# Rotary halves swapped by transfers, and norm factors spread through DRAM, in a fused attention, state-space and expert layer

## The chip, the cores and the metric

The kernel runs on one NeuronCore of a Trainium2 chip. Time is device microseconds (us) of one execution; less is better. The engines named below are TensorE (PE, with its weight loads as PEld), VectorE (DVE), ScalarE (ACT), GpSimd (POOL) and SyncE (SP), which here only issues transfers.

## The reference, cut to what matters

One decoder layer over 512 tokens of width 1024. The part that the change touches is the latent attention: two RMS norms of narrow latents, and a rotary embedding of queries and keys.

```python
def rms_norm(x, g):
    xf = x.astype(jnp.float32)
    return (xf * lax.rsqrt(jnp.mean(xf * xf, -1, keepdims=True) + NORM_EPS) * g).astype(x.dtype)

def apply_rope(x, cos, sin):
    x1, x2 = jnp.split(x.astype(jnp.float32), 2, axis=-1)
    return jnp.concatenate([x1 * cos - x2 * sin, x2 * cos + x1 * sin], axis=-1).astype(x.dtype)

def mla_heads(q_lat, kv_lat, k_pe, cos, sin, q_norm_g, w_q_b, kv_norm_g, w_kv_b):
    q = (rms_norm(q_lat, q_norm_g) @ w_q_b).reshape(B, S, MLA_HEADS, MLA_NOPE_DIM + MLA_ROPE_DIM)
    q_nope = q[..., :MLA_NOPE_DIM]
    q_pe = apply_rope(q[..., MLA_NOPE_DIM:], cos[:, None], sin[:, None])
    kv = (rms_norm(kv_lat, kv_norm_g) @ w_kv_b).reshape(B, S, MLA_HEADS, MLA_NOPE_DIM + MLA_V_DIM)
    k_nope, v = kv[..., :MLA_NOPE_DIM], kv[..., MLA_NOPE_DIM:]
    k_pe = apply_rope(k_pe, cos, sin)
    ...   # scores = q_nope k_nope + q_pe k_pe, causal softmax, times v
```

The rest of the layer: a LayerNorm, one input projection, a causal convolution, a chunked state-space product (SSD, 16 heads), an output projection, a second LayerNorm, and an expert mixer (PEER) over 16,384 experts. There are 8 attention heads, each with 128 plain and 64 rotary features.

## The kernel before, in words

Everything is written as an instruction order by hand: each engine runs its own queue in the order of the code, and waits on semaphores only. Activations lie with features on the 128 partitions and the 512 tokens along a row. Weights stream in by SP as raw tiles `wir`; ACT rounds each to a high part `wih` (L122), DVE or POOL subtracts for the low part `wil` (L132), and each product is three matmuls (L85, L86, L87: high by high, low by high, high by low).

The stages that matter here, with their places in the profiled execution:

- **Input projection (to 137 us).** The loop over `i` makes 18 blocks of 128 features in PSUM tiles `pa`. Block 0 holds the rotary key (rows 0 to 63 of `kd`) and the time steps; blocks 1 to 12 go through the convolution on DVE (L388, L390); blocks 13 to 15 are the query latent, 16 and 17 the key/value latent. At `i == 3`, `k_rope` makes the rotary key: two matmuls with 0/1 matrices (L600, L601) put the key twice over the partitions, plain and with its halves swapped, and `rope` (L593 to L595 on DVE) multiplies by cosine and sine and adds.
- **Latent norms.** `lat_a(15)` and `lat_a(17)` sum squares over the partitions with a matmul that leaves one factor for each token, token on partition, and take the inverse root on DVE (a chain of twelve small operations). Four DVE operations (L659) spread the factors on a diagonal, and in `lat_b` a matmul with ones (L664) copies them to every partition. `lat_b` then scales each latent block on DVE (L667), rounds on ACT (L669) and subtracts on DVE (L670).
- **Gate projection (the loop over `n`, 137 to 195 us).** Eight weight tiles make `zt`. Between them stands work of the state-space part (`do`): `ssd_s` makes states (L544, read by DVE at L546), `ssd_off` their outputs (L518, read by DVE at L521), `ssd_y` the products inside a chunk (L530, read at L534). All of their PSUM results are four rotating tiles `pb`.
- **Attention (from 198 us).** A pair of heads `p` takes its rotary queries from `q_pe(p)`, a generator with two halves. The first makes a product in a PSUM tile and scales it into `qx` (L752 on ACT for pair 0, L750 on DVE for the others). The second, in `before`, multiplies `qx` by a permutation matrix (L756), runs `rope` (L593 to L595), rounds on ACT into `qph` (L760) and subtracts into `qpl` on DVE (L761); POOL then copies both into the operands `q` by four transfers (L764). `scores` reads them at L814, for pair `p` first at head `2p`. Thirty-nine steps `st` run the heads one after the other, four query blocks each: `scores`, DVE's row maximum (L818), ACT's exponential (L826), scaling, transposes (L845), an evacuation by ACT and DVE (L736 `thh`, L737 `thl`) and the product with `v` (`po`). Each step also advances the generator of the next heads' operands once.

The names `pt`, `pu`, `po` are PSUM tiles of the attention.

Of the kernel before, what the change touches and what calls it, by code (L numbers as in the profile page):

```python
# [11 lines left out]
F32 = mybir.dt.float32  # L12
# [6 lines left out]
OP = mybir.AluOpType  # L19
# [4 lines left out]
S = 512  # L24
D = 1024
NB = 4
# [30 lines left out]
BIG = 1.5 * 2.0 ** 26  # L57
GG = 48 - UG // 8

C_COS, C_SIN, C_PQ, C_END = 0, 512, 1024, 1152  # L60
T_TRI, T_DK, T_RK, T_END = 0, 128, 256, 384

P_CW, P_CB, P_LG, P_LB, P_QG, P_KG, P_SG, P_END = 0, 48, 60, 68, 76, 79, 81, 89

# [2 lines left out]
def tile_block(ctx: ExitStack, tc: tile.TileContext, I, out):  # L67
    nc = tc.nc
    ctx.enter_context(tc.manual_schedule())
    V, A, T, G = nc.vector, nc.scalar, nc.tensor, nc.gpsimd  # L70
# [141 lines left out]
    C = cs2.tile([128, C_END], F32, name="C")  # L212
    PAR = cs2.tile([128, P_END], F32, name="PAR")
    HR = cs2.tile([128, 48], F32, name="HR")
    ident = cs2.tile([128, 128], F32, name="ident")
# [12 lines left out]
    dram = pool("dram", space=DRAM)  # L228
    xsp = dram.tile([NB, 128, D], F32, name="xsp")
    gsp = dram.tile([NT // 32, 128, 128, 32], F32, name="gsp")  # L230
    acd = dram.tile([64, 128], F32, name="acd")
    asp = dram.tile([PRE - KEEP, 128, NU], F32, name="asp")

    wst = pool("wst")
# [6 lines left out]
    wk = pool("wk")  # L241
    CT = wk.tile([128, T_END], F32, name="CT")
    tri = CT[:, T_TRI:T_TRI + 128]
    ntm = wk.tile([128, 128], BF16, name="ntm")
    ones = wk.tile([128, 128], F32, name="ones")
# [7 lines left out]
    pb = lambda: psB.tile([128, 512], F32, name="pb")  # L253
# [48 lines left out]
    for p in range(2):  # L302
# [7 lines left out]
        rs = sqrt_rs(lnp, mv4[:, bs, 1], [128, 2], f"l{p}", eps)  # L310
# [57 lines left out]
    kd = wk.tile([128, S], F32, name="kd")  # L368
# [10 lines left out]
    cu, co = {}, {}  # L379
# [211 lines left out]
    def rope(pool_, px, prot, tag, bufs):  # L591
        a = pool_.tile([128, S], F32, name=tag, bufs=bufs)
        V.tensor_tensor(a, px, cosT, op=OP.mult)  # L593
        V.tensor_tensor(prot, prot, sinT, op=OP.mult)
        V.tensor_tensor(a, a, prot, op=OP.add)  # L595
        return a

    def k_rope():
        p1, p2 = pb(), pb()
        T.matmul(p1, CT[0:64, T_DK:T_DK + 128], kd[0:64], start=True, stop=True)  # L600
        T.matmul(p2, CT[0:64, T_RK:T_RK + 128], kd[0:64], start=True, stop=True)  # L601
        kr = rope(wk, p1, p2, "co", 2)
        A.activation(kpe[0], kr, AF.Copy)
        V.tensor_tensor(kpe[1], kr, kpe[0], op=OP.subtract)

    dp = dt_prep()
    for i in range(13):
        ps = proj(i)
        if i == 0:
            A.activation(kd[0:80], ps[0:80], AF.Copy)  # L610
        else:
            conv_a(i, ps)
        if i >= 2:
            conv_b(i - 1)
        if i >= 5:
            conv_c(i - 2)
        if i in (4, 5):
            conv_c(i - 3)
        if i in (2, 4, 6, 7, 9):
            next(dp)  # L620
        if i == 3:
            k_rope()
        if i == 11:
            ssd_m(0, 0)
        if i == 12:
            ssd_cb(0)
            ssd_m(0, 1)
# [19 lines left out]
    sqs, lrs = {}, {}  # L647

    def lat_a(i):
        m = 3 if i == 15 else 2  # L650
        ps = pb()
        for b in range(NB):
            T.matmul(ps[:, b:b + 1], sqs[i][:, b * 128:(b + 1) * 128], ones[:, 0:1], start=True, stop=True)
        v = lat.tile([128, NB], F32, name="lv", bufs=2)
        V.tensor_scalar(v, ps[:, 0:NB], 1.0 / (128 * m), EPS, op0=OP.mult, op1=OP.add)
        rs = rsqrt(lat, v, [128, NB], "ls")
        dg = wk.tile([128, S], F32, name="co", bufs=2)
        for b in range(NB):
            V.tensor_scalar(dg[:, b * 128:(b + 1) * 128], ident, rs[:, b:b + 1], None, op0=OP.mult)  # L659
        lrs[i] = dg  # L660

    def lat_b(i):
        ps = pb()
        T.matmul(ps, ones, lrs[i], start=True, stop=True)  # L664
        lo, hi, g0, oh, ol = (0, 3, P_QG, qlh, qll) if i == 15 else (3, 5, P_KG, kvh, kvl)
        for m in range(lo, hi):
            V.scalar_tensor_tensor(qraw[m], qraw[m], PAR[:, g0 + m - lo:g0 + m - lo + 1], ps,  # L667
                                   op0=OP.mult, op1=OP.mult)
            A.activation(oh[:, m - lo], qraw[m], AF.Copy)  # L669
            V.tensor_tensor(ol[:, m - lo], qraw[m], oh[:, m - lo], op=OP.subtract)  # L670

    for i in range(13, 18):
        ps = proj(i)
        if i == 16:
            lat_a(15)
        q = qraw[i - 13] = wk.tile([128, S], F32, name="qr", bufs=5)
        A.activation(q, ps, AF.Copy)
        sqs[i] = wk.tile([128, S], F32, name="ca", bufs=3)
        A.activation(sqs[i], ps, AF.Square)
        if i not in (13, 16):  # L680
            V.tensor_tensor(sqs[i], sqs[i], sqs[i - 1], op=OP.add)
        do(i - 13)
        if i == 17:
            lat_b(15)


    for n in range(8):
        hf, kp = divmod(n, 4)
        if kp == 0:
            acc = [pa() for _ in range(4)]  # L690
        h, l = item()
        for kk in range(2):
            k = kp * 2 + kk
            wh, wl = h[:, kk * 512:(kk + 1) * 512], l[:, kk * 512:(kk + 1) * 512]
            for b in range(NB):
                bs = slice(b * 128, (b + 1) * 128)
                mm3(acc[b], HH[:, k, bs], HL[:, k, bs], wh, wl, k == 0, k == 7)
        if kp == 3:
            for b in range(NB):
                A.activation(zt[:, b, hf * 512:(hf + 1) * 512], acc[b], AF.Silu)  # L700
        if n == 1:
            lat_a(17)
        if n == 4:
            lat_b(17)
        do(n + 5)
# [23 lines left out]
    pp = pu  # L729
# [12 lines left out]
    def q_pe(p):  # L742
        wh, wl = item()
        ps = pp()
        for k in range(3):
            ks = slice(k * 128, k * 128 + 128)
            mm3(ps, wh[:, ks], wl[:, ks], qlh[:, k], qll[:, k], k == 0, k == 2)
        qx = ml.tile([128, S], F32, name="qx")
        if p:
            V.tensor_scalar(qx, ps, SCALE, None, op0=OP.mult)  # L750
        else:
            A.activation(qx, ps, AF.Copy, scale=SCALE)  # L752
        win.splits(cnt[0] + 1)
        yield
        pr = pp()
        T.matmul(pr, C[:, C_PQ:C_PQ + 128], qx, start=True, stop=True)  # L756
        a = rope(ml, qx, pr, "rp", 1)
        q2 = [ml.tile([128, S], F32R, name=f"q2{e}", bufs=2) for e in range(2)]
        qp = [ml.tile([128, S], F32R, name="qp" + n) for n in "hl"]
        A.activation(qp[0], a, AF.Copy)  # L760
        V.tensor_tensor(qp[1], a, qp[0], op=OP.subtract)  # L761
        for e in range(2):
            for x in (e, 1 - e):
                G.dma_start(q2[e][x * 64:x * 64 + 64], qp[e ^ x][e * 64:e * 64 + 64])  # L764
            QP[2 * p + e] = q2[e]
# [107 lines left out]
            w_out_mm(acc, b, k, hl)  # L873

    gq, gk = q_pe(0), qk_nope(0, pk=pt)
    for g in (gq, gk, gq, gk, gk):
        next(g, None)
    g = chain(qk_nope(1, pq=pt), v_proj(0))
    for _ in range(2):
# [919 lines left out]
def _host(inp):  # L1799
# [31 lines left out]
    ch[:, 0:256] = np.repeat(r, 2)  # L1831
    ch[:, 256:512] = np.repeat(np.arange(16), 16)
    o["ch"] = ch
    rot = (r // 64) * 64 + (r % 64 + 32) % 64
    c[rot, C_PQ + r] = 1
    c1[r % 64, T_DK + r] = 1
    c1[rot % 64, T_RK + r] = 1
    o["cst1"] = c1
    inv = (10000.0 ** (-np.arange(32) / 32.0)).astype(f)
    ang = (np.arange(S, dtype=f)[:, None] * inv).astype(np.float64)  # L1840
# [37 lines left out]
```

## Time and profile before

| what | value |
|---|---|
| median of 3 runs | 1547.5 us (1543.41 to 1547.81) |
| the profiled execution | 1544.92 us, of which the span is 1543.0 us |
| granted TensorE clock, mean | 0.998 |
| busy share of the span | PE 99%, PEld 87%, DVE 88%, ACT 49%, POOL 41% |
| chain that ended last | PE 83%, DVE 7%, DMA 4%, ACT 3% |

The busy share says how much of the span an engine had an instruction in flight; matmuls overlap, so 99% is not a statement that nothing waited. The chain that ended last is followed back from the last instruction, at each step to what released it.

### The profile page before, as it was taken

The page shows a single profiled execution, that of the slowest core. Times are in us where ns is not written, and L with a number is a line of the kernel's source. Part 1 is how long each engine was busy: PE and PEld are TensorE (multiplying, and loading weights), DVE is VectorE, ACT ScalarE, POOL GpSimd, SP SyncE. Part 2 cuts the span into 40 slices and gives each one's busy share as a digit, 9 for nine tenths or more (in the row PEclk, how much of TensorE's full clock was granted, in tenths as well). Part 3 has the DMA queues.
Part 4 walks back from the last instruction along what each step waited for, and adds up shares of the span by engine and source line. Part 5 has one row for each costly group of instructions (what it writes and reads, how often), then busy time and mean ns, then how long its engine had stood idle before and what let it go on. Part 6 is the DMA issues. An engine that isn't in the chain of part 4 may idle for free.

```text
span 1543.0 us, 24619 instructions
## 1 busy us (share of the span) xinstructions
PE 1522.6 (99%) x8696; PEld 1338.1 (87%) x8696; DVE 1354.0 (88%) x2611; ACT 761.2 (49%) x1415; POOL 634.6 (41%) x466
## 2 busy tenths in 40 slices
PE   9999999999999999999999999999999999999997
PEld 7787888888888999999999889999999888888885
DVE  8979768655799999999998599988999999999997
ACT  5574476742333444667667544444443344444442
POOL 0000032420044522435430476656666766776610
PEclk9999999999999999999999999999999999999999
DMA  6242122375322566999998999999999999999983
GB/s 258 96 149 99 57 71 59 104 252 164 127 76 90 150 209 215 346 343 348 383 329 288 366 402 389 392 387 375 386 398 399 394 390 375 385 385 379 377 285 138
DMA packets 153403, 417.19 MB, mean 270 GB/s; under 512 B 15440, under 2 KB 56544, under 8 KB 153024
## 3 DMA queue, kind: packets, MB, share of 16 engines
q1 hardware_dynamic: 95568, 210.11, 39.1%
q0 software_dynamic: 52304, 187.08, 32.6%
q10 hardware_dynamic: 5408, 18.43, 3.0%
q8 instruction: 68, 1.11, 0.3%
q14 instruction: 55, 0.45, 0.1%
HBM read 383.36 MB, written 30.05 MB: 268 GB/s over the span
## 4 chain that ended last, share of the span: by engine, by line
PE 83%; DVE 7%; DMA 4%; ACT 3%; issue 2%; POOL 1%; DVEq 0%; ACTq 0%; POOLq 0%
PE pu L85 10%; PE va L1669 9%; PE va L1672 9%; PE va L1668 9%; PE pu L87 9%; PE pu L86 9%; PE pa L87 3%; PE pa L86 3%; PE pa L85 3%; PE pw L86 3%; PE pw L87 3%; PE pw L85 3%; DMA row<-v,ix 2%; PE pw L1268 1%; PE pw L1269 1%
## 5 line engine op out<-in xcount | busy, mean ns | idle before, releaser
L122 ACT ACTIVATE wih<-wir 128x1024 fp32r<-128x1024 f32 (+2 forms) x269 | 277.7, 1033 | 220.7 <-DMA wir<-ut 112.8
L132 DVE TENSOR_TENSOR wil<-wir,wih 128x1024 fp32r<-128x1024 f32 (+1 forms) x234 | 282.9, 1210 | 66.3 <-ACT wih L122 49.2
L87 PE MATMUL pu<-XT,wil 128*128 128x320 f32 x1008 | 311.6, 309 | 0.1
L1669 PE MATMUL va<-wil,Ph 128*128 128x512 f32 x726 | 283.0, 390 | 0.0
L85 PE MATMUL pu<-XT,wih 128*128 128x320 f32 x840 | 262.2, 312 | 1.3 <-ACT aout L1411 1.3
L1535 POOL DMA_INDIRECT row<-v,ix x128 | 220.4, 1722 | 99.4 <-DVE ac L1556 82.9
L86 PE MATMUL pu<-XT,wih 128*128 128x320 f32 x840 | 259.5, 309 | 0.0
L1535 POOL DMA_INDIRECT row<-u,ix x128 | 176.2, 1376 | 137.3 <-DVE row L1550 74.4
L87 PEld LDWEIGHTS pu<-XT,wil 128*128 128x128 f32 x1008 | 189.2, 188 | 0.4 <-DVE wil L132 0.4
L1668 PE MATMUL va<-wih,Ph 128*128 128x512 f32 x480 | 186.8, 389 | 0.0
L1556 DVE SCALAR_TENSOR_TENSOR ac<-row,hd,ac 128x1024 f32<-128x1024 f32 x128 | 164.1, 1282 | 2.4 <-DMA row<-v,ix 0.8
L1550 DVE SCALAR_TENSOR_TENSOR row<-row,XT 128x1024 f32<-128x1024 f32 x128 | 153.2, 1221 | 9.2 <-DMA row<-u,ix 8.9
L85 PEld LDWEIGHTS pu<-XT,wih 128*128 128x128 f32 x840 | 157.7, 188 | 3.4 <-ACT aout L1411 1.6
L1669 PEld LDWEIGHTS va<-wil,Ph 128*128 128x128 f32 x726 | 136.2, 188 | 26.9
L86 PEld LDWEIGHTS pu<-XT,wih 128*128 128x128 f32 x840 | 157.8, 188 | 1.6
L1132 POOL DMA_INDIRECT urow<-u,uix x64 | 97.6, 1525 | 138.6 <-DVE urow L1138 122.1
L1672 PE MATMUL va<-wih,Pl 128*128 128x512 f32 x480 | 147.9, 389 | 0.0
L132 POOL TENSOR_TENSOR wil<-wir,wih 128x1024 fp32r<-128x1024 f32 (+3 forms) x35 | 72.8, 2088 | 154.0 <-PE pw L87 99.4
L1651 ACT ACTIVATE Ph<-P 128x384 fp32r<-128x384 f32 x121 | 62.7, 518 | 125.7 <-DVE P L1628 107.8
L1672 PEld LDWEIGHTS va<-wih,Pl 128*128 128x128 f32 x480 | 90.1, 188 | 18.9
L1668 PEld LDWEIGHTS va<-wih,Ph 128*128 128x128 f32 x480 | 90.1, 188 | 18.1
L122 ACT ACTIVATE wihx<-wir 128x1024 fp32r<-128x1024 f32 x67 | 71.0, 1060 | 60.4 <-DMA wir<-v 33.1
(508 smaller groups left out, 3325.1 us busy)
## 6 DMA issues: line engine op xcount, KB each, us to landing
wir<-ut SPq DMA_DIRECT2D x128, 512.0 KB, 6.6
wir<-v SPq DMA_DIRECT2D x128, 512.0 KB, 6.9
gt<-gsp SPq DMA_DIRECT2D x63, 256.0 KB, 8.7
wir<-wo SPq DMA_DIRECT2D x26, 512.0 KB, 3.6
gsp<-stg ACTq DMA_DIRECT2D x21, 448.0 KB, 7.0
wir<-wf SPq DMA_DIRECT2D x18, 512.0 KB, 3.4
wir<-wqr SPq DMA_DIRECT2D x16, 512.0 KB, 3.7
asp<-aout SPq DMA_DIRECT2D x34, 160.0 KB, 6.0
```

The costliest lines, as they stand in the source:

```text
L85: T.matmul(ps, lh, rh, start=start, stop=False)
L86: T.matmul(ps, lh, rl, start=False, stop=False)
L87: T.matmul(ps, ll, rh, start=False, stop=stop)
L122: A.activation(h, r, AF.Copy)
L132: self.lo(n).tensor_tensor(l, r, h, op=OP.subtract)
L1132: G.indirect_dma_start(out=UR[n], out_offset=None, in_=I["u"], in_offset=bass.IndirectOffsetOnAxis(ap=UR["ix"][:, n:n + 1], axis=0))
L1535: G.indirect_dma_start(out=R[s], out_offset=None, in_=I["u"] if s < 128 else I["v"], in_offset=bass.IndirectOffsetOnAxis(ap=ix3[:, s % 128 ...
L1550: V.scalar_tensor_tensor(wide(r), wide(r), 1.0, x3, op0=OP.mult, op1=OP.mult, accum_out=hd[:, s:s + 1])
L1556: V.scalar_tensor_tensor(ac, r, hd[:, s - 128:s - 127], ac, op0=OP.mult, op1=OP.add)
L1668: T.matmul(va[b][e], Ph[b], h[:, cs], start=c == 0, stop=False)
L1669: T.matmul(va[b][e], Ph[b], l[:, cs], start=False, stop=False)
L1672: T.matmul(va[b][e], Pl[b], h[:, cs], start=False, stop=c == 127)
```

## The change

Three edits belong together. The 0/1 matrices and the eight float32 matmuls of 512 columns that used them or spread the factors are gone; transfers do their work.

- **Key.** After block 0 is copied to `kd`, POOL issues six transfers (`k_copies`) that fill two tiles with the key twice over the partitions, plain and with halves swapped. `rope` at `i == 3` reads these.
- **Norm factors.** `lat_a` writes its factors to a small DRAM tensor by one POOL transfer of single elements (128 partitions by 4), and a second POOL transfer reads them back as a row to all 128 partitions. `lat_b(15)` moves from the end of `i == 17` to `n == 1`, ahead of `lat_a(17)`.
- **Queries.** After `qx`, SP issues four transfers of 32 partitions each, which write `qx` with swapped halves into a tile `qr`; `rope` reads that. At the entry of the attention, the second half of `qk_nope(0)` (the key product and its evacuation) is advanced ahead of the second half of `q_pe(0)`.

```diff
+    kk = {}
+
+    def k_copies():
+        kk["a"], kk["b"] = (wk.tile([128, S], F32, name="qr", bufs=5) for _ in range(2))
+        for x in range(2):
+            G.dma_start(kk["a"][x * 64:x * 64 + 64], kd[0:64])
+        for x in range(4):
+            G.dma_start(kk["b"][x * 32:x * 32 + 32], kd[32 - x % 2 * 32:64 - x % 2 * 32])
+
     def k_rope():
-        p1, p2 = pb(), pb()
-        T.matmul(p1, CT[0:64, T_DK:T_DK + 128], kd[0:64], start=True, stop=True)
-        T.matmul(p2, CT[0:64, T_RK:T_RK + 128], kd[0:64], start=True, stop=True)
-        kr = rope(wk, p1, p2, "co", 2)
+        kr = rope(wk, kk["a"], kk["b"], "co", 2)
...
             A.activation(kd[0:80], ps[0:80], AF.Copy)
+            k_copies()
...
-        dg = wk.tile([128, S], F32, name="co", bufs=2)
-        for b in range(NB):
-            V.tensor_scalar(dg[:, b * 128:(b + 1) * 128], ident, rs[:, b:b + 1], None, op0=OP.mult)
-        lrs[i] = dg
+        dg = lrs[i] = wk.tile([128, S], F32, name="co", bufs=2)
+        d = lrd[i != 15]
+        G.dma_start(d.rearrange("b p -> p b"), rs)
+        G.dma_start(dg, d.rearrange("b p -> (b p)")[None, :].to_broadcast([128, S]))
 
     def lat_b(i):
-        ps = pb()
-        T.matmul(ps, ones, lrs[i], start=True, stop=True)
+        ps = lrs.pop(i)
...
-        if i == 17:
-            lat_b(15)
...
         if n == 1:
+            lat_b(15)
             lat_a(17)
...
+        pr = ml.tile([128, S], F32, name="qr")
+        for x in range(4):
+            nc.sync.dma_start(pr[x * 32:x * 32 + 32], qx[(x ^ 1) * 32:(x ^ 1) * 32 + 32])
         win.splits(cnt[0] + 1)
         yield
-        pr = pp()
-        T.matmul(pr, C[:, C_PQ:C_PQ + 128], qx, start=True, stop=True)
         a = rope(ml, qx, pr, "rp", 1)
...
-    for g in (gq, gk, gq, gk, gk):
+    for g in (gq, gk, gk, gq, gk):
         next(g, None)
```

On DVE, the scaling of the query latent (`qr`, with `qll` its low part) stood between the state-space work of `i == 17` and the first state update of the gate projection (`prev`). Before:

```order
L495 TENSOR_TENSOR de<-de,cbT 128x1024
L667 SCALAR_TENSOR_TENSOR qr<-qr,PAR,pb 128x512
L670 TENSOR_TENSOR qll<-qr,qlh 128x512
L667 SCALAR_TENSOR_TENSOR qr<-qr,PAR,pb 128x512
L670 TENSOR_TENSOR qll<-qr,qlh 128x512
L667 SCALAR_TENSOR_TENSOR qr<-qr,PAR,pb 128x512
L670 TENSOR_TENSOR qll<-qr,qlh 128x512
L132 TENSOR_TENSOR wil<-wir,wih 128x1024
L541 TENSOR_TENSOR prev<-prev,cdec 128x1024
L546 TENSOR_TENSOR prev<-prev,pb 128x512 x2
```

In the changed kernel the state update follows at once, and the scaling stands later on DVE, ahead of the chain of `lat_a(17)` (whose first row is `lv`), which in turn stands ahead of the reading of `ssd_off` (L522 there, L521 before). Rows from the state update on, with those between left out:

```order
L496 TENSOR_TENSOR de<-de,cbT 128x1024
L132 TENSOR_TENSOR wil<-wir,wih 128x1024
L542 TENSOR_TENSOR prev<-prev,cdec 128x1024
L547 TENSOR_TENSOR prev<-prev,pb 128x512 x2
...
L674 SCALAR_TENSOR_TENSOR qr<-qr,PAR,co 128x512
L677 TENSOR_TENSOR qll<-qr,qlh 128x512
...
L663 TENSOR_SCALAR lv<-pb 128x4
...
L522 TENSOR_TENSOR cu<-pb,eac 128x512
```

So the six rows of the scaling moved behind the state update and in front of the two rows that empty `ssd_off`'s PSUM tiles.

On SP, in the attention, the raw weight tiles stood one behind the other. In the changed kernel four transfers of each pair stand between them (pairs 0 and 1 shown, `qr` is the swapped tile):

```order
L104 DMA wir<-wqkv 128x640
L760 DMA qr<-qx 32x512 x4
L104 DMA wir<-wqkv 128x640
L104 DMA wir<-wqkv 128x512
L104 DMA wir<-wqkv 128x384
L760 DMA qr<-qx 32x512 x4
```

The transfers of a pair wait for `qx`; the next weight tile is issued behind them.

## Rows read from the trace of the kernel before

**Rows 1.** Busy time by stretch: window, PE, PEld, DVE, ACT, POOL, clock, DMA.
```profile
108.00:170.00 62.00, 61.57 (x313) 49.23 (x311) 57.42 (x100) 32.18 (x70) 2.12 (x4) 1.00 0.32 105
200.00:286.00 86.00, 84.45 (x500) 70.66 (x499) 64.89 (x150) 59.99 (x141) 27.38 (x30) 1.00 0.28 74
```

**Rows 2.** The chain that ended last, to 320 us: start, us, what.
```profile
39.09 1.05 PE pb L600 x2
40.15 0.86 PE pb L601 x2
...
175.75 0.86 PE pb L664 x2
```

**Rows 3.** Timeline around the rotary key, DVE and PE: start, us, instruction.
```profile
38.47 1.22 DVE L132 TENSOR_TENSOR wil<-wir,wih 128x1024 fp32r<-128x1024 f32 x1
...
47.22 0.68 DVE L593 TENSOR_TENSOR co<-pb,C 128x512 f32<-128x512 f32 x1
...
50.88 1.23 DVE L132 TENSOR_TENSOR wil<-wir,wih 128x1024 fp32r<-128x1024 f32 x1 [0.26 <-ACT wih L122]
...
53.35 0.40 PE L87 MATMUL pa<-HH,wil 128*128 128x512 f32 x1
```

**Rows 4.** Timeline of the gate projection, DVE and then PE.
```profile
138.97 0.74 DVE L667 SCALAR_TENSOR_TENSOR qr<-qr,PAR,pb 128x512 f32<-128x512 f32 x1
...
144.51 0.69 DVE L670 TENSOR_TENSOR qll<-qr,qlh 128x512 fp32r<-128x512 f32 x1 [0.70 <-ACT qlh L669]
...
147.92 1.29 DVE L546 TENSOR_TENSOR prev<-prev,pb 128x512 f32<-128x512 f32 x2
...
159.36 0.69 DVE L521 TENSOR_TENSOR cu<-pb,eac 128x512 f32<-128x512 f32 x1
...
143.61 1.02 PE L544 MATMUL pb<-xdw,btok 128*128 128x512 f32 x2
...
159.34 3.73 PE L530 MATMUL pb<-xdt,de 128*128 128x128 f32 x32
```

**Rows 5.** Timeline at the attention's entry, all engines.
```profile
200.50 0.60 ACT L752 ACTIVATE qx<-pu 128x512 f32<-128x512 f32 x1
...
204.38 0.69 DVE L594 TENSOR_TENSOR pu<-pu,C 128x512 f32<-128x512 f32 x1
...
204.60 0.40 PE L85 MATMUL pt<-qlh,wih 128*128 128x512 f32 x1
...
207.48 0.52 POOL L764 DMA_DIRECT2D q<-qpl  x1 [0.20 <-issue]
...
210.00 0.47 PE L814 MATMUL pt<-kpe,q 128*128 128x256 f32 x2
```

**Rows 6.** Timeline of pair 1, DVE and PE.
```profile
217.86 0.69 DVE L750 TENSOR_SCALAR qx<-pu 128x512 f32<-128x512 f32 x1 [0.70 <-PE pu L87]
...
219.77 0.70 DVE L594 TENSOR_TENSOR pu<-pu,C 128x512 f32<-128x512 f32 x1 [0.23 <-PE pu L756]
...
224.67 0.69 DVE L737 TENSOR_TENSOR thl<-pt,thh 128x512 fp32r<-128x512 f32 x1 [0.63 <-ACT thh L736]
...
226.26 0.39 PE L86 MATMUL po<-thl,vh 128*128 128x512 f32 x1
```

**Rows 7.** Timeline of pair 2, DVE and PE.
```profile
242.96 0.68 DVE L750 TENSOR_SCALAR qx<-pu 128x512 f32<-128x512 f32 x1
...
247.02 0.69 DVE L594 TENSOR_TENSOR pu<-pu,C 128x512 f32<-128x512 f32 x1
...
252.54 0.50 PE L86 MATMUL po<-thl,vh 128*128 128x512 f32 x1 [0.21 <-DVE thl L737]
```

**Rows 8.** Transfers: four issues in a row on SP; to landing; query operands' landing.
```profile
0.75 1.81 SPq L281 DMA_DIRECT2D XH<-x  x4
...
wir<-wqkv SPq DMA_DIRECT2D x4, 192.0 KB, 2.3
...
DMA to landing us min/median/max: 2.2/2.7/4.0
```

More of the change, by code (lines that the diff above doesn't have):

```diff
@@ L58 @@
 GG = 48 - UG // 8
-C_COS, C_SIN, C_PQ, C_END = 0, 512, 1024, 1152
-T_TRI, T_DK, T_RK, T_END = 0, 128, 256, 384
+C_COS, C_SIN, C_END = 0, 512, 1024
+T_TRI, T_END = 0, 128
 P_CW, P_CB, P_LG, P_LB, P_QG, P_KG, P_SG, P_END = 0, 48, 60, 68, 76, 79, 81, 89
@@ L231, in tile_block @@
     acd = dram.tile([64, 128], F32, name="acd")
+    lrd = [dram.tile([NB, 128], F32, name=f"lrd{j}") for j in range(2)]
     asp = dram.tile([PRE - KEEP, 128, NU], F32, name="asp")
@@ L1833, in _host @@
     o["ch"] = ch
[L1834 to L1837, printed above, removed]
     o["cst1"] = c1
```

## The prediction

> **What bounds the kernel now.** I read the chain that ended last first, then busy time by stretch, then the timeline around every place that the diff touches. The chain is 83% PE, and PE has work in flight for 61.57 of 62.00 us in the gate projection's stretch and for 84.45 of 86.00 in the first heads of the attention [rows 1]. So a matmul taken out of PE's queue pays its price at that moment. The reader should see one more number in the same rows: DVE is busy for 57.42 of those 62 us and for 64.89 of the 86. It has little room to follow a PE that comes earlier, and each edit makes DVE wait for something new or moves work on it. The prediction therefore turns on DVE's timeline.
>
> **What is removed.** Eight float32 matmuls of 512 columns: two for the key, two for the norm factors, four permutations. On the chain the key's pair costs 1.05 and 0.86, a norm factor's 0.86 [rows 2]; I price all others at 0.86. That is 1.05 + 7 x 0.86 = 7.1 us, and 7.4 if two more of them carry the 0.19 by which the first of the key's pair is longer. Also gone are four diagonal operations of DVE for each factor row.
>
> **Key: 1.2 gained of 1.9.** The next projection would start at 39.1 instead of 41.0. DVE is not ready for that: its low weight tile ends at 38.47 + 1.22 = 39.69 [rows 3], and the third matmul, at about 39.4, reads it: 0.35 lost. Some blocks on, L87 stands at 53.35 and its tile `wil` is ready at 50.88 + 1.23 = 52.11; with 1.9 gained less 0.25 it would start near 51.7, so 0.45 more is lost. Left: 1.91 - 0.35 - 0.45 = 1.1, say 1.2 as the first loss covers part of the second. The six copies are issued by POOL, about 0.52 each [rows 5], from some 36.6, and land at most 4.0 after issue [rows 8]: near 44. `rope` reads them at 47.22 [rows 3], hence nothing. Without this cover (a landing of 7) each further us would stop DVE.
>
> **Norm factors: 0.** Two L664 are 1.72 gained. The six DVE rows of `lat_b(15)` run from 138.97 to 144.51 + 0.69 = 145.2, waits for ACT included: 6.2 us [rows 4]. In front of L546 they cost nothing: taken out there, DVE can start L546 only when PE's L544 has given its first product, at about 143.61 - 0.86 + 1.02 = 143.8, 4.1 before the 147.92 of now. But they come back whole ahead of L521. L521 then starts at 159.36 - 4.1 + 6.2, less 0.9 for the diagonal operations and some 0.25 of waits: about 160.6 to 160.9, so 1.3 to 1.5 later. PE is 0.86 early and begins its 32 small products at 158.48 (now 159.34). They fill four rotating PSUM tiles at 0.93 each, 3.73 in all [rows 4]; the third takes the tile that the first L521 empties, at 160.86 + 0.69 = 161.55. PE gets there at 160.3 and waits 1.3, the fourth 0.4 more behind the second L521. 1.7 lost against 1.72 gained. The factors' own transfers have cover: about 22 us for block 15, and for block 17 from just before 159.36 to its reader, which now stands at 175.75 [rows 2], 16 us. Two transfers in a row at the longest landing, 4.0 [rows 8], are 8 us.
>
> **Query swap: what it takes.** Four SP issues in a row take 1.81, 0.45 each [rows 8]. The last lands 3 x 0.46 + 0.1 + landing after `qx`. Nothing in this trace moves 64 KB from SBUF to SBUF on SP; the nearest rows are the weight tiles on SP with 2.3 (larger, from DRAM) and the query operands on POOL with 2.2, 2.7 and 4.0 at least, in the median and at most [rows 8]. I take 2.3, since SP issues here and nothing else but one weight tile at a time is in flight: 3.8 from the end of `qx` to the operand. Ends: 3.7 (landing 2.2) and 5.5 (4.0).
>
> **Pair 0: 1.3 lost.** `qx` is done at 201.10 [rows 5], and SP has a weight tile ahead until some 201.8; swapped halves are there near 205.4. But the key product now stands ahead on PE and its evacuation ahead of `rope` on DVE: that product ends at 204.60 - 0.86 = 203.74 [rows 5], then ACT 0.6, DVE 0.69 and the cosine product 0.68, so the sine product starts at about 205.65 whatever the transfer does up to there, against 204.38. That is 1.27 later; the last operand copies follow, at 207.48 + 1.27 = 208.75. L814 stands at 210.00, 2.52 behind the 207.48 issue: it waits for that landing, not for PE [rows 5]. So it comes at 211.27, 1.3 later, and PE's gain of 0.86 drowns in the wait.
>
> **Pair 1: 1.7 lost.** `qx` ends at 217.86 + 0.69 = 218.55; 3.8 later is 222.35, and the sine product stood at 219.77 [rows 6]: 2.58 late. DVE is in order, so behind it wait the maxima and scalings of the running head and the evacuation `thl`. That ended at 224.67 + 0.69 = 225.36, will end at 227.94, and L86 reads it. L86 stood at 226.26 [rows 6], so 1.68 of the 2.58 reaches PE after the 0.90 of slack, and the 0.86 saved is inside that.
>
> **Pairs 2 and 3: 0.9 lost.** In pair 2, `qx` ends at 243.64, 3.8 later is 247.44, against 247.02 [rows 7]: 0.42 late. PE already waits for `thl` there (L86 at 252.54 names it as its releaser [rows 7]), so the delay passes through and the permutation's 0.86 is not seen. Pair 3 has the same pattern; I take 0.5.
>
> **Sum.** +1.2 + 0 - 1.3 - 1.7 - 0.4 - 0.5 = 2.7 us slower. The profiled execution took 1544.92, so 1547.6. The runs shown stand between 1543.41 and 1547.81, and the four times have a mean of 1545.9; from that the sum gives **1548.5**, my prediction. A measurement of this kernel can tell about 0.3%, 4.6 us, from no change: this forecast lies inside. Its own range: with a landing of 2.2 nearly the same, 2.3 lost; with the median of 2.7, pairs 1 to 3 lose 0.4 more each, 4 in all; if the slot wait of the norm factors doesn't happen, 1 lost. 1546 to 1551.
>
> A rule speaks on the four issues. Four copies of a pair's operands, issued 0.52 apart, all land 2.2 to 4.0 after their own issue [rows 5, 8], though each lasts longer than the distance of the issues: they overlap. The Trainium skill (DMA: Bandwidth & Descriptors, Rules for kernel authors) holds that two transfers to disjoint partition halves run one after the other and that one transfer over 128 partitions is to be used. This case's trace disagrees for transfers of another shape; the swap's shape it does not show. With the rule the price is that of rival C.
>
> **The rivals.**
>
> A, faster: all eight matmuls pay. It needs DVE not to be late anywhere: swap transfers that land within 1.5 us behind the last issue, and the gap ahead of L521 closed by waits of DVE's that shrink. For it: in most of its rows PE is what others wait for [rows 2]. Against it: the slot and operand waits above, and no row with a landing under 2.2. 1545.9 - 7.4 = 1538.5. If only pairs 1 to 3 are hidden and the key pays whole, 2 to 3 faster: no measurable change.
>
> B, slower: the swap is late by its landing. At 4.0 each instead of 2.3, pair 1's DVE waits 4.3 instead of 2.6, pairs 2 and 3 are later by the same 1.7 each, and pair 0 is reached too (swapped halves at 207.1 against 205.65: 1.45). 2.7 + 3 x 1.7 + 1.5 = 9.3: 1555.2. For it: query operand copies of this size do reach 4.0 [rows 8], and the weight tiles go through the same queue. It decides (over 4.6 slower) from a landing of about 2.8 for all four pairs.
>
> C, slower: the four transfers run one after the other, 4 x 2.3 = 9.2 instead of 3.8, 5.5 more in each of four pairs: 2.7 + 22 = some 25, 1571. Against it: the overlap told above.
>
> D: the change does what it says on PE, but the waits that it meets are shorter than worked out, by chance of the slack at later heads: between 0 and 4 faster, 1542 to 1546.
>
> **How the numbers follow.** Forecast 0.46, of which 0.05 lies over 4.6 slower; A 0.16; B 0.20, with all between it and the forecast; C 0.03; D 0.15, hardly any of it over 4.6 faster. Faster: 0.16 of A and 0.01 of D, 0.17. Slower: 0.05 + 0.20 + 0.03 = 0.28. Same: 0.55. For 8 in 10 I leave out C, the lower half of A and the outer part of B: 1539.5 to 1555.5.
>
> **What would show it.** In the profile after: the first matmul of the projection behind the key at 39 with a wait for `wil` at its third; PE idle by 1 to 2 us inside the small products L531, released by DVE's reading of `ssd_off` (L522); the four swaps of a pair with issue-to-landing of 2.2 to 2.7; DVE idle ahead of the sine product (L595), 2 to 3 us in pair 1 and under 1 us in pairs 2 and 3; PE idle by about 2 us at the first rotary scores (L820); `thl` as the releaser of `po` products behind each pair. Wrong would be: no PE gap at L531 (then the norm factors paid 1.7); key copies that land after 47 (then the key costs); the weight tile behind the swaps late on SP, which I priced at nothing since the tiles are loaded well ahead; or gaps of PE at some place that I did not name, above all where a PSUM tile that the removed matmuls had used now comes round to another user, and changes whom PE waits for.

## The result: 0.8% slower, and the profile after

The changed kernel takes 1561.87 us in the median of five runs (1555.25 to 1562.26) against 1546.88 for the kernel before: ratio 1.008, 95% interval 1.0062 to 1.0097, some 12 us. The forecast was 1548.5, range 1539.5 to 1555.5. The profiled execution is the fastest of the five, 1555.25 at a mean granted clock of 0.997; of the other four three show 0.994 and one, at 1562.10, shows 0.997 as well.

From the page of the changed kernel, busy shares and the chain that ended last:

```profile
PE 1520.7 (98%) x8680; PEld 1336.6 (86%) x8680; DVE 1354.0 (87%) x2603; ACT 759.5 (49%) x1415; POOL 639.4 (41%) x476
...
PE 74%; DVE 15%; DMA 3%; ACT 3%; issue 2%; POOL 1%; SPq 0%; DVEq 0%; ACTq 0%; POOLq 0%
```

PE works 1.9 us less and yet the span is 10.5 us longer. The chain went from 83% PE and 7% DVE to 74% and 15%: more of the chain now runs through DVE. The timeline of the changed kernel on PE (start, us, instruction, idle time before it and its releaser) shows where, at the instructions that the prediction spoke of:

```profile
51.99 0.50 PE L87 MATMUL pa<-HH,wil 128*128 128x512 f32 x1 [0.29 <-DVE cu L386]
...
160.28 0.38 PE L531 MATMUL pb<-xdt,de 128*128 128x128 f32 x1 [1.06 <-DVE cu L522]
...
161.61 0.38 PE L531 MATMUL pb<-xdt,de 128*128 128x128 f32 x1 [0.17 <-DVE cu L522]
...
212.10 0.39 PE L820 MATMUL pt<-kpe,q 128*128 128x256 f32 x1 [4.05 <-DMA q<-qpl]
...
231.71 0.51 PE L86 MATMUL po<-thl,vh 128*128 128x512 f32 x1 [0.23 <-DVE thl L742]
...
259.62 0.50 PE L86 MATMUL po<-thl,vh 128*128 128x512 f32 x1 [0.23 <-DVE thl L742]
...
292.39 0.33 PE L851 MATMUL pt<-ident,P 128*128 128x128 f32 x1 [0.97 <-DVE thl L742]
```

The last of them in the trace of before:

```profile
284.32 0.33 PE L845 MATMUL pt<-ident,P 128*128 128x128 f32 x1 [0.35 <-DVE thl L737]
```

Read against [rows 3] and [rows 5 to 7], the changed kernel stands 1.36 us ahead at L87 (53.35), 2.10 behind at the first rotary scores (210.00), 5.45 behind after pair 1 (226.26), 7.08 behind after pair 2 (252.54) and 8.07 behind after pair 3. At the first transposes behind the output projection, just ahead of the expert mixer, it is 8.70 behind, before and after:

```profile
386.52 1.03 PE L976 MATMUL px<-ident,xm 128*128 128x128 f32 x8
...
395.22 1.03 PE L982 MATMUL px<-ident,xm 128*128 128x128 f32 x8
```

I call this place the mark; the experiments use it to see what the part up to there costs. The large steps are pair 0 and what follows on it up to pair 1. Pair 0's rows on ACT, SP, DVE and POOL:

```profile
199.38 0.60 ACT L757 ACTIVATE qx<-pu 128x512 f32<-128x512 f32 x1
...
201.38 2.73 SPq L760 DMA_DIRECT2D qr<-qx  x4
...
205.54 0.69 DVE L595 TENSOR_TENSOR qr<-qr,C 128x512 f32<-128x512 f32 x1 [0.81 <-DMA qr<-qx]
...
208.64 0.54 POOL L770 DMA_DIRECT2D q<-qpl  x1 [0.19 <-issue]
...
208.85 0.33 SPq L104 DMA_DIRECT2D wir<-wqkv  x1
```

`qx` is ready at 199.98, but the first swap is issued 1.40 us later and the four issues take 2.73 (0.45 each was forecast). Then the second operand copy, issued at 208.64, is waited for until 212.10: 3.46, not the 2.52 of before. A weight tile (128 x 512) is issued 0.2 us behind it; before, it came 0.8 behind.

And there is something that the prediction had no term for. Busy time by stretch (length, then PE, PEld, DVE, ACT, POOL, granted clock, DMA share, GB/s):

```profile
208.00:212.10 4.10, 0.05 (x2) 0.00 (x1) 2.71 (x5) 2.12 (x5) 3.82 (x6) 1.00 0.73 181
212.10:213.00 0.90, 0.90 (x7) 0.85 (x8) 0.29 (x1) 0.00 (x0) 0.90 (x1) 0.98 0.37 69
213.00:216.40 3.40, 3.40 (x17) 3.31 (x16) 0.73 (x3) 1.33 (x2) 3.40 (x4) 0.50 0.17 53
216.40:220.00 3.60, 3.60 (x22) 2.87 (x22) 2.49 (x9) 3.20 (x10) 0.41 (x1) 1.00 0.00 0
```

PE idles for 4 us, works for 0.9, and is then granted 0.50 of its clock, 1.2 GHz, for 3.40 us: 1.7 us of work lost behind a wait that was already paid. Before, the clock in these stretches is 1.00 [rows 1]; its trace is at 0.50 only from 1537.9 on, when PE has done its last matmul (1534.3), and that alone makes its mean of 0.998. Not every idle stretch is followed by it: in the same trace PE works 1.62 us of four ahead of 232, and the clock stays (length, PE, granted clock, DMA share, GB/s):

```profile
228.00:232.00 4.00, 1.62 (x7) 1.00 0.50 104
232.00:236.00 4.00, 4.00 (x24) 1.00 0.44 115
```

### The profile page after: what moved, and what is told of

It is laid out like the page before. It is cut to its first block, busy times and chain, and to the rows that moved or that the text cites. A ratio compares the mean times of both kernels' runs of the same rounds, so it can differ in the third digit from the quotient of the medians.

```text
span 1553.5 us, 24636 instructions
## 1 busy us (share of the span) xinstructions
PE 1520.7 (98%) x8680; PEld 1336.6 (86%) x8680; DVE 1354.0 (87%) x2603; ACT 759.5 (49%) x1415; POOL 639.4 (41%) x476
## 4 chain that ended last, share of the span: by engine, by line
PE 74%; DVE 15%; DMA 3%; ACT 3%; issue 2%; POOL 1%; SPq 0%; DVEq 0%; ACTq 0%; POOLq 0%
PE va L1675 10%; PE va L1674 10%; PE va L1678 10%; PE pu L85 9%; PE pu L87 8%; PE pu L86 8%; PE pa L87 2%; PE pa L85 2%; PE pa L86 2%; DMA wir<-ut 2%; DVE t L1024 1%; PE pw L86 1%; PE pw L87 1%; PE pw L85 1%; DVE wil L132 1%
## 5 line engine op out<-in xcount | busy, mean ns | idle before, releaser
L87 PE MATMUL pu<-XT,wil 128*128 128x320 f32 x1008 | 311.6, 309 | 0.0
L1541 POOL DMA_INDIRECT row<-v,ix x128 | 216.1, 1689 | 104.4 <-DVE ac L1562 87.9
L87 PEld LDWEIGHTS pu<-XT,wil 128*128 128x128 f32 x1008 | 189.2, 188 | 0.2 <-DVE wil L132 0.2
```

The lines of the kernel that those rows point to most:

```text
L87: T.matmul(ps, ll, rh, start=False, stop=stop)
L1541: G.indirect_dma_start(out=R[s], out_offset=None, in_=I["u"] if s < 128 else I["v"], in_offset=bass.IndirectOffsetOnAxis(ap=ix3[:, s % 128 ...
```

## The experiments

Each ratio is to runs of the kernel before on the same chip, with its 95% interval.

**1. The parts.** Three runs split the change: key and factors alone, queries alone, and pair 0 alone put back.

```diff
 # e1_key_factors: after, with the queries of before
+        pr = pp()
+        T.matmul(pr, C[:, C_PQ:C_PQ + 128], qx, start=True, stop=True)
...
+    for g in (gq, gk, gq, gk, gk):
 # e2_queries: before, with the swaps and the entry order of after
 # e3_pair0_mm: after, but
+        if not p:
+            pr = pp()
+            T.matmul(pr, C[:, C_PQ:C_PQ + 128], qx, start=True, stop=True)
...
+    for g in (gq, gk, gq, gk, gk):
```

> The key and the norm factors by transfers, the queries by permutation matmuls in the order of before. Theory (the whole loss comes from the query swaps): the key gives 1.4 us, the factors give and lose 1.7, so 1545.5 us, ratio 0.999, mean granted clock 0.998 as before. Rival (the transfers of key and factors share in the loss, by POOL and the queues they occupy): 1550 or more.

> Only the query swaps and their order, put into the kernel before. Theory: all of the loss and the 1.4 of the key on top, 1563 us, ratio 1.0105, PE idle for 4 us ahead of the first rotary scores and half clock behind it. Rival (loss shared with key and factors): 1553 to 1556, ratio 1.005.

> The changed kernel with pair 0 alone back on its permutation matmul and in the order of before; pairs 1 to 3 keep their swaps. Theory (pair 0's stall of 4 us and the half clock behind it are the larger part): about 1549 us, clock 0.998 in every execution. Rival (each pair costs its quarter of the 15 us): 1558.

Measured: key and factors 0.9994 (0.9981 to 1.0006), clock 0.997 to 0.999; queries 1.0073 (1.0052 to 1.0094), between what the theory and the rival expect; with pair 0 back 1.004 (1.0023 to 1.0058), also between them. So the loss is the queries', with some 0.4% for pair 0 (1.008 less 1.004) and some 0.46% for pairs 1 to 3 (1.004 less 0.9994), each to within about 0.25%. The mark in the traces, key and factors first, then with pair 0 put back:

```profile
385.38 1.03 PE L981 MATMUL px<-ident,xm 128*128 128x128 f32 x8
...
391.58 1.03 PE L986 MATMUL px<-ident,xm 128*128 128x128 f32 x8
```

Against 386.52 before and 395.22 after, that is 1.14 ahead and 5.06 behind: in these executions pair 0 has 3.6 us and pairs 1 to 3 have 6.2. The clock did not come back with pair 0: half-clock stretches follow pairs 1 and 2 in that trace (0.57 in 4 us each), and another stands far behind the attention, from 758.9 us. The first by stretch:

```profile
222.00:226.00 4.00, 2.27 (x12) 1.44 (x10) 3.23 (x7) 2.82 (x8) 1.61 (x3) 1.00 0.16 33
226.00:230.00 4.00, 3.48 (x12) 2.75 (x13) 3.46 (x8) 2.69 (x8) 2.08 (x2) 0.57 0.62 131
```

PE had worked 2.27 of 4.00 us, while the sine product of pair 1 waited for its swap on DVE.

**2. PE kept at work in pair 0's wait.**

```diff
+        if (h, qb) == (0, 0):
+            for _ in range(8):
+                T.matmul(ps[:, 0:256], ident, cosT[:, 0:256], start=True, stop=True)
         mm3(ps[:, :n], q[0][:, qs], q[1][:, qs], k[0][:, :n], k[1][:, :n], True, False)
```

> The changed kernel with eight float32 matmuls of 256 columns, whose result nobody reads, ahead of the first scores, so that PE works in most of the 4 us that it waits for the query operands. The wait stays. Theory (the idle time brings the clock down, for longer in the executions above 1560 than in the profiled one): no half clock behind the wait, 1553 to 1554 in all executions, clock 0.998. Rival (the lower mean clock of the 1560 us executions has nothing to do with that wait): still about 1560, clock 0.994.

Measured: 1.0081 (1.006 to 1.0103), nothing gained, the time that the rival gives. The half clock behind pair 0 is gone in the profile, but one stands behind pair 2, and another at 1245.6 in the expert mixer:

```profile
212.00:217.00 5.00, 4.41 (x31) 4.04 (x32) 1.32 (x3) 2.27 (x5) 5.00 (x5) 1.00 0.33 80
258.50:262.60 4.10, 3.84 (x13) 3.14 (x14) 3.65 (x8) 2.60 (x7) 1.48 (x1) 0.58 0.64 156
```

The theory's time did not come. Whether the wait brings the clock down is not decided by it, since later stalls remain.

**3. No swaps at all, and the order at the entry.** The runs without swaps leave out a part of the rotary embedding: the sine product reads the operand with its halves unswapped.

```diff
 # e5_noswap: after, without the four transfers
-        for x in range(4):
-            nc.sync.dma_start(pr[x * 32:x * 32 + 32], qx[(x ^ 1) * 32:(x ^ 1) * 32 + 32])
...
+        a = rope(ml, qx, qx, "rp", 1)
 # e9_order_alone: before, but
+    for g in (gq, gk, gk, gq, gk):
 # e10_noswap_order0 = e5_noswap, e11_order0 = after, both with
+    for g in (gq, gk, gq, gk, gk):
 # e12_noswap_filled: e5_noswap with the eight matmuls of experiment 2
```

> The changed kernel without the query swaps: the sine product reads the unswapped operand (that part of the rotary embedding is left out); order and all else as in the changed kernel. Theory (nothing but the wait for the swaps, with the PE idle time and half clock that follow, makes the queries slow): key -1.2, four permutations -0.86 each, about 5 us faster than before, ratio 0.997, clock 0.998, no half clock in the attention. Rival (the changed order at the entry, with the key's evacuation ahead of the rotary products, costs by itself): ratio 1.001 or more, with PE still idle ahead of the first rotary scores by over 1 us.

Measured: 1.0044 (1.0029 to 1.0059). My theory fell: with no swap to wait for, PE still waited 3.99 us ahead of the first rotary scores, and the granted clock was 0.78 over 208 to 213, 0.50 over 213 to 217 and 0.92 over 217 to 221, which is half the clock for 0.22 x 2 x 5 + 4 + 0.08 x 2 x 4 = 6.8 us, of which some 1.1 lie still in the wait. The second copy, issued at 207.76, was there at 211.93: 4.17 later, with the weight tile issued 0.20 behind it. That led to a new theory, and in the trace of before I found what I had read past. Landing of the operand copies that were issued there at 206.75 and 207.48, and of those at 207.99 and 208.50, with the weight tile at 208.28:

```profile
DMA to landing us min/median/max: 2.2/2.3/2.4
...
DMA to landing us min/median/max: 3.7/3.9/4.0
```

The 4.0 of [rows 8] was no scatter of landings: it belongs to copies that ran beside the weight tile. The entry order takes the key's evacuation out from between the last operand (`qpl`) and the weight tile's subtraction on DVE, which frees the buffer that SP loads next. So the tile comes 0.6 us sooner after the copies, and, as I read it, the second copy falls among its packets. Four runs on this:

> The kernel before with one edit: at the attention's entry the key product and its evacuation are advanced ahead of the second half of pair 0's queries, as in the changed kernel; all matmuls stay. Theory (new): the evacuation that stood between the last operand of the query copies and the next weight tile's subtraction on DVE is gone from there, so SP issues that weight tile (256 KB) right behind the first copies, and its packets delay the second copy to 4 us from issue; with the rotary products 1.3 us later PE waits some 3 us ahead of the first rotary scores: ratio 1.002 to 1.004, a half clock stretch in some executions. Rival (the order costs nothing by itself, only the missing matmuls and the swaps do): ratio 1.000 to 1.001, L814 waits under 1.3 us.

> The run without the swaps (the sine product reads the unswapped operand) in the order of before at the entry. Theory (new): the second copy lands some 2.5 us from issue and ahead of the weight tile, PE waits about 1 us instead of 4 ahead of the first rotary scores, no half clock there, ratio 0.997 to 0.999 against 1.0044 with the changed order. Rival (PE's wait comes from the missing permutation matmul alone): still 3 us or more, ratio 1.003.

> The changed kernel, swaps and all, with the order of before at the entry. Theory (new): the sine product still waits for the swap and stays at about 205.5, but the second copy is ahead of the weight tile and lands 2.5 us from issue: PE's wait falls from 4.0 to some 3, and the time by 1 us or, where the half clock goes too, by 3: ratio 1.006 to 1.007. Rival (the swap's wait sets everything): 1.008, with DVE's key evacuation later and no gain.

> The run without the swaps in the changed order, with the eight unused float32 matmuls of 256 columns ahead of the first scores: PE waits as long, but works meanwhile. Pairs 1 to 3 have no swap here, so no later stall can bring the clock down instead. Theory (the idle 4 us are what halves the clock behind them): no half clock in the attention, ratio 1.0044 less 2.8 us, 1.0026, and clock 0.998 in most executions. Rival (the half clock has another cause, such as the load before): half clock at the same place, 1.0044.

Measured: the order alone, all matmuls in place, 1.003 (1.0012 to 1.0048). Its timeline on POOL, SP and PE:

```profile
208.68 0.52 POOL L764 DMA_DIRECT2D q<-qpl  x1 [0.20 <-issue]
...
208.88 0.33 SPq L104 DMA_DIRECT2D wir<-wqkv  x1
...
212.50 0.36 PE L814 MATMUL pt<-kpe,q 128*128 128x256 f32 x1 [2.67 <-DMA q<-qpl]
```

Without swaps and in the order of before, 1.0008 (0.9993 to 1.0023):

```profile
206.42 0.54 POOL L767 DMA_DIRECT2D q<-qpl  x1 [0.19 <-issue]
...
207.22 0.33 SPq L104 DMA_DIRECT2D wir<-wqkv  x1
...
208.92 0.38 PE L817 MATMUL pt<-kpe,q 128*128 128x256 f32 x1 [0.93 <-DMA q<-qpl]
```

With the tile 0.20 us behind the copy it takes 3.82, with the tile 0.80 behind it 2.50, as the theory has it. It is so in every trace of this case: the second copy lands after 2.4 to 2.5 in the nine with the order of before (tile 0.80 behind it), and is there after 3.5 to 4.4 in the eight with the changed one (0.20 behind). No run moved the tile alone, so that its packets are the cause stays argued. The order alone shows no half clock in its profile: the clock is 1.00 behind its wait of 2.67. But of its twelve executions the four with a mean clock of 0.998 or more take 1546.96 to 1550.58, and the eight with less 1550.45 to 1559.78.

The ratio 1.0008 is above the 0.997 to 0.999 expected; the interval reaches down to 0.9993, so the gain of four missing permutations, 3.4 us, did not show.

Without swaps, in the changed order and with PE kept at work: 1.0008 (0.9993 to 1.0023), against 1.0044 with PE idle. By stretch and at the mark, first without and then with the eight matmuls:

```profile
208.00:213.00 5.00, 1.07 (x5) 0.97 (x6) 1.93 (x4) 1.24 (x3) 4.92 (x6) 0.78 0.88 197
213.00:217.00 4.00, 4.00 (x20) 3.91 (x20) 0.99 (x3) 1.42 (x2) 2.89 (x3) 0.50 0.00 0
...
390.42 1.03 PE L979 MATMUL px<-ident,xm 128*128 128x128 f32 x8
```

```profile
208.00:213.00 5.00, 4.26 (x24) 3.62 (x23) 2.07 (x5) 1.45 (x3) 4.91 (x6) 1.00 0.88 195
213.00:217.00 4.00, 4.00 (x29) 3.54 (x28) 1.42 (x4) 2.51 (x5) 3.15 (x3) 1.00 0.01 2
...
388.34 1.03 PE L982 MATMUL px<-ident,xm 128*128 128x128 f32 x8
```

The scores come at 212.35 there, no sooner than 211.93: the wait is the same, the clock is not. The ratios differ by 0.36%, 5.6 us, to within some 0.2%, and in the traces the filled one is 2.1 us ahead at the mark. So the 2.8 us expected are borne out, and that the clock is worth more is not shown. Work that nobody reads made the kernel faster. So here it is the idle time, not the load before it, that brings the clock down.

The changed kernel in the order of before: 1.0082 (1.0059 to 1.0105), as the rival has it, though the interval just reaches the theory's 1.006 to 1.007. The second copy lands after 2.5 us and PE waits for it 1.65 instead of 4.05, but the granted clock is 0.57 over 212 to 216, again 0.58 over 259.5 to 263.5 behind pair 2, and 0.50 from 1246.6 for 3.4 us. With the swaps still there, putting the order right does not show.

**4. The norm factors' 1.7 us, and two issuing queues.**

```diff
 # e6_lat15: after, but
-            lat_b(15)
             lat_a(17)
...
+        if n == 5:
+            lat_b(15)
 # e7_two_queues: after, but
-            nc.sync.dma_start(pr[x * 32:x * 32 + 32], qx[(x ^ 1) * 32:(x ^ 1) * 32 + 32])
+            (nc.sync, nc.scalar)[x % 2].dma_start(pr[x * 32:x * 32 + 32], qx[(x ^ 1) * 32:(x ^ 1) * 32 + 32])
```

(The factors of block 15 then lie in a tile of another ring, since they live longer.)

> The changed kernel with the scaling of the query latent moved further down, from n == 1 to the end of n == 5, where DVE idles. Theory (the 1.7 us of PE waits among the small products of ssd_y come from that scaling standing ahead of the reading of ssd_off's tiles): those waits go, PE is 1.7 us earlier at the attention's entry, and the time falls from ratio 1.008 to 1.007. Rival (the tiles are late for another reason): the waits stay.

> The changed kernel with the four swap transfers of a pair issued by SP and ACT in turn instead of all by SP. Theory (four issues of 0.6 to 0.8 us in a row are a good part of the swap's 5.5 us in pair 0 and 3.9 in the others): the last transfer lands 1.2 us earlier, PE's wait ahead of the first rotary scores falls from 4.0 to 2.8, the waits behind pairs 1 to 3 fall too; ratio 1.005. Rival (the landing sets the delay, or transfers run one after the other whatever queue they come from): no change, 1.008.

Measured: with the scaling moved, the 32 small products run without a wait (start 157.25, all 32 in 3.74 us), as expected, and PE is 1.8 us earlier at the attention (195.23 against 197.02); the time is 1.0079 (1.0056 to 1.0102), where that gain can't be told from noise. Two queues: 1.0092 (1.0068 to 1.0116), no better than 1.008 and perhaps worse, as the rival has it, though for another reason. The sine product's waits for swaps fell from 5.8 us in all to 2.0, but ACT does no other work for 2.43 and 2.60 us in pairs 1 and 2, some 1.0 in wait for `qx` and 1.42 for its two issues, and in pair 0 the second copy takes 3.78 us.

**5. Swaps that nobody waits for, and the best version.**

```diff
 # e13_early: e3_pair0_mm, but
+        if q == 3 and h in (0, 2, 4):
+            gq = q_pe(h // 2 + 1)
+            next(gq)
...
 # e14_early_lat15: that, with lat_b(15) at n == 5
 # e15_pairs23: e13_early with the matmul in pairs 0 and 1
 # e8_best: e1_key_factors with lat_b(15) at n == 5
```

> Pair 0 on its permutation matmul and in the order of before, pairs 1 to 3 by swaps, but their products and scaled operands are made one step earlier (at the end of the preceding head), the rotary products where they were: the swap has a whole step of 3 us or more in addition. Theory (DVE standing in its queue for the swap, and the half clock behind that, are all that pairs 1 to 3 cost): no wait of the sine product, ratio 1.004 falls to 0.998 (three permutations of 0.86 gained besides the key's 1.2). Rival (the transfers cost by their issues on SP, which hold the weight tiles up, or by their traffic): ratio 1.002 or more.

> The same with the scaling of the query latent at the end of n == 5. Theory: the gains add up, key 1.2, factors 1.7, three permutations up to 2.6: 4 to 5.5 us faster than before, ratio 0.9965, better than the 0.9976 of the version without swaps. Rival (PE waits for the evacuation of the transposed probabilities there anyway, so the permutations' time does not come back): 0.998.

> As the run with the products one step earlier, but pair 1, the only one whose sine product still waited for its swap (2.4 us), is back on its permutation matmul too: swaps in pairs 2 and 3 alone, none of them waited for. Theory (waits for the swap are what costs): no slower than the version without any swap, ratio 0.998 to 0.9995. Rival (issues on SP and traffic cost by themselves): 1.001 or more.

> Key and norm factors by transfers with the scaling of the query latent at the end of n == 5, queries by permutation matmuls as before. Theory: key 1.2 and factors 1.7 gained, nothing lost, 3 us faster than before, ratio 0.998, clock 0.998. Rival (what PE gains ahead of the attention is lost at later waits): ratio 1.000.

Measured: 1.0024 (1.0011 to 1.0036) for the earlier products, against 1.004 and as the rival has it; the sine product's waits fell from 5.4 us in three pairs to 2.4 in pair 1 alone, so the theory's condition, no wait, was not met. With the scaling moved as well 1.0003 (0.9994 to 1.0013), above theory and rival (0.9965 and 0.998). With pair 1 on its matmul too 1.000 (0.9982 to 1.0017), with one wait of 1.5 us left: between theory and rival, and the interval holds both. Key and factors alone, with the scaling at `n == 5`: 0.9976 (0.9964 to 0.9988), 3 us expected and 3.7 measured. This version beats both kernels, and it has no query swap.

## Why the prediction was wrong, by its own steps

**Key: right.** 1.2 forecast, 1.36 at L87 (51.99 against 53.35), with a wait of 0.29 there, and 0.21 at the third matmul behind the key, the two places that were named. (The releaser printed, `cu`, is a memset of 0.06 us that stands on DVE right behind the `wil` that was named.) The copies were early enough.

**Norm factors: right in the time, wrong in the cover.** The waits of PE stand where they were put, at the third and fourth tile, released by DVE's reading of `ssd_off`, and go when the scaling moves; they sum to 1.23, where 1.7 was forecast. But the transfers take twice what I allowed. POOL's rows for block 15, DVE's first row for block 17, and the landing of the four:

```profile
128.45 0.78 POOL L667 DMA_DIRECT2D lrd<-lsy  x1 [16.20 <-DVE lsy L151]
139.57 0.55 POOL L668 DMA_DIRECT2D co<-lrd  x1 [10.34 <-DMA lrd<-lsy]
...
175.56 0.75 DVE L674 SCALAR_TENSOR_TENSOR qr<-qr,PAR,co 128x512 f32<-128x512 f32 x1 [0.18 <-DMA co<-lrd]
...
DMA to landing us min/median/max: 5.1/7.7/10.8
```

The scatter of 512 single elements lands up to 10.8 us from issue and the read 5.1 at the least, 16 where "8 us" stood; block 17's 16 us of cover were short by the 0.18 that DVE waited. The Trainium skill (DMA: Bandwidth & Descriptors, Rules for kernel authors) says that a last dimension that is not contiguous becomes one descriptor for each element; the 10.8 us fit that, though no row here shows the descriptors.

**Pair 0: the step that failed.** "the last operand copies follow ... it waits for that landing": I gave the second copy the 2.52 us of before, though the reordering that I described changes what SP issues beside it. The run with the order alone shows that step by itself: there the second copy is issued at 208.68, where the prediction puts it at 208.75, and the scores come at 212.50, not 211.27, since the copy takes 3.82. It costs 0.3%. In the changed kernel PE was already 1.1 us ahead there (`qx` at 199.98 for 201.10), which the sum counts under the key; with that the forecast of L820 is 211.27 - 1.1 = 210.2. It came at 212.10. Of the 1.9, 1.0 is the swap (sine product at 205.54 instead of 204.55: the first issue 0.7 later, four issues 0.9 longer, some of it in time that DVE did not need), 0.9 the copy that ran beside the weight tile (3.46 for 2.52).

One reading under this term was wrong, too. L814 did not wait for the landing in the kernel before: it follows on PE's matmul without idle time, and the copy was there 2.4 us after its issue, at 209.9.

```profile
209.75 0.28 PE L87 MATMUL pt<-knh,qnl 128*128 128x256 f32 x1
```

So PE and the copy came out within 0.2 us of each other by chance, and the 2.52 holds that much of PE's own time.

**Missing: the clock.** The prediction had PE idle by about 2 us at the first rotary scores; it was 4.05, and no term said that half the clock may follow on a wait. It was put at nothing without a reason. In the profiled execution that is 1.7 us; the runs without swaps show 2.1 us at the mark, and 5.6 with the wide margin told above in the times. The lower clocks of three of the other executions (0.994, by 0.003 x 2 x 1555 some 9 us more at half clock, 4.7 us lost) are of the size by which they exceed the profiled one, 5.2 to 7.0. That is an inference, as only the profiled one has a trace here, and the execution of 1562.10 at 0.997 exceeds it by 6.85 with no lower clock, so it isn't the whole of it.

**Pair 1: right in size.** The wait for the swap was forecast as 2.58 later at the sine product and 1.7 on PE. Rows on SP and DVE, pairs 1 to 3:

```profile
222.25 0.51 SPq L760 DMA_DIRECT2D qr<-qx  x1
...
226.19 0.69 DVE L595 TENSOR_TENSOR qr<-qr,C 128x512 f32<-128x512 f32 x1 [2.98 <-DMA qr<-qx]
...
254.09 0.69 DVE L595 TENSOR_TENSOR qr<-qr,C 128x512 f32<-128x512 f32 x1 [1.18 <-DMA qr<-qx]
...
283.84 0.69 DVE L595 TENSOR_TENSOR qr<-qr,C 128x512 f32<-128x512 f32 x1 [0.89 <-DMA qr<-qx]
```

From `qx` to the sine product it took 3.97 us (3.8 forecast). The end of `qx` stands 3.67 behind (222.22 against 218.55), 1.6 more than the 2.10 of the scores, which is the half clock's share; on PE, 5.45 less 3.67 leaves 1.8 for pair 1, 1.7 forecast.

**Pairs 2 and 3: too small.** 0.4 and 0.5 forecast; 1.6 (7.08 - 5.45) and 1.0 (8.07 - 7.08) measured. DVE waits 1.18 and 0.89: the issues are 0.63 apart and not 0.46, and in pair 2 the sine product starts 2.8 us behind the last issue, in pair 1 2.1.

**The tally.** After pair 3 the forecast has the changed kernel 2.7 behind, the trace 8.07. Of the 5.4 between, pair 0 has 2.0 (0.1 forecast, key and pair 0 together, 2.10 measured), the clock 1.6, pair 1 0.1, pairs 2 and 3 have 1.7. (The sum itself was rounded: 1545.9 and 2.7 are 1548.6.)

**The rivals.** None was it. B had the sign, but by a landing of 4.0 for the swaps; that was 1.9 to 3.1, 2.0 in the median, and the operand copies that it called "of this size" carry 128 KB where a swap transfer carries 64. C, with the rule of the Trainium skill (DMA: Bandwidth & Descriptors, Rules for kernel authors) that two transfers to disjoint partition halves run one after the other, was not seen: issued 0.6 apart, the last is used 2 to 3 us after its own issue. None had the clock.

**Open.** Behind pair 3 the two traces drift another 2.4 us apart (10.5 of span), 0.6 of it ahead of the mark. The rest arises in the expert mixer, and the trace of key and factors alone, no slower in the runs, loses 3.0 there (1.14 ahead at the mark, 1.9 above in span), so I don't count it to the change; its cause stays open. How the 0.46% of pairs 1 to 3 divide between wait and clock is not shown: no run kept PE at work there. Why the permutations' time does not come back is seen in part. Without swaps and in the order of before PE stands 2.0 us ahead at its last matmul before the rotary scores, waits 0.93 for the second copy, and at the mark it is here:

```profile
385.02 1.04 PE L979 MATMUL px<-ident,xm 128*128 128x128 f32 x8
```

That is 1.5 ahead, and key and factors alone give 1.14 of it. So four missing permutations left 0.4 us of 3.4 at the mark; where pairs 1 to 3 give the rest away is not shown.

## What to carry to other kernels

A matmul on a full PE is dear at 0.86 us, but the transfers in its place put 4 to 5.6 us in front of what reads them here, and an in-order engine that stands there holds up all that is queued behind it. Price a stall of PE with the half clock that may follow, and where several stalls stand close, do not count on mending one: here it showed nothing twice (1.0081 and 1.0082), and only all of pair 0 put back gave some 0.4%. When an edit reorders instructions, look which transfer it releases, and beside which latency-bound copy that one will run.

## What the runs showed of the hardware

- A 4 us wait of PE came with 3.4 us at a granted clock of 0.50 behind it, or with 6.8 that began some 1.1 us ahead of its end; eight matmuls without use in that wait kept it at 1.00. A wait of 2.67 us (the order alone) and 1.62 us of work in 4.00 (pair 1 of the changed kernel) were not followed by a half clock in their traces; 2.27 in 4.00 (with pair 0 put back) was. The Trainium skill (TensorE: Matmul & The Clock Gate, HAM oscillation — how this bites in real kernels) tells of a kernel whose PE falls to half rate because it waits for transfers; the 0.50 behind the 4.05 us wait here agrees.
- A 128 KB operand copy on POOL's queue lands 2.2 to 2.5 us from issue when the weight tile is issued 0.80 us or more behind it, and is there after 3.5 to 4.4 when that 256 KB tile is issued on SP 0.2 us behind it. The Trainium skill (DMA: Bandwidth & Descriptors, Queues, rings and completion order) says that each DMA engine takes packets from its queues in turn; the longer landing fits that, and no run here shows the packets' order.
- Four issues on SP of 32-partition transfers from SBUF to SBUF take 2.4 to 2.7 us in the changed kernel (2.73 in pair 0), against 1.81 for the four at the start of the program [rows 8]. They overlap: each landed 1.9 to 3.1 us from its own issue.
